# Adaptive max pooling over 16-element windows: a flat input in two groups, longer reductions, and one extra load to 16 partitions

## The chip, the cores and the metric

The kernel runs on one NeuronCore of a Trainium2 chip. The metric is the time of one execution on the device in microseconds (us). The kernel before takes 336.05 us, the median of 10 runs that lie between 335.86 and 336.18.

## The reference

The input `x` is float32 of 32 x 256 x 4096, 134.2 MB. The output is 32 x 256 x 256, 8.4 MB. Output column `i` is the maximum over 16 consecutive input elements, since 4096 / 256 = 16:

```python
for i in range(output_size):
    start = int(i * length / output_size)
    end = int((i + 1) * length / output_size)
    result[:, :, i] = np.max(x[:, :, start:end], axis=-1)
```

Every window is 64 contiguous bytes of the input and gives 4 bytes of the output. In memory both are one long row of 2,097,152 windows, so any cut of that row at a window's edge gives a valid tiling.

## The kernel before, in words

The 8192 rows of 4096 elements (16 KB each) are cut into three groups of 21 rows on each of the 128 partitions, and a rest of 128 rows, one on each partition. Within a group, partition `p` holds 21 neighbouring rows, so the distance in HBM between what two neighbouring partitions read (the pitch) is 21 x 16 KB = 336 KB.

One load (line 59, issued by SyncE, SP) brings 3 rows to each partition, 48 KB in one piece, 6,291,456 bytes in all. It goes into three of the nine places of a ring in SBUF, so the ring holds three loads. VectorE (DVE) then runs one `reduce_max` for each of the three rows (line 53): 128 partitions x 256 windows of 16 elements. The results of a group are gathered in a tile `out` of its own. There are 7 loads in a group and 21 in the three groups. The rest is one load of 16 KB to each partition (line 68), and its result goes into a place of the ring (`spare`).

The order is that of the program; the framework only adds the waits. SP issues its transfers in program order: a load waits until the reductions that read its place in the ring are done. All loads come first. After the last load SP issues the stores of the first two groups (line 72), then the third group's store in two pieces, 15 rows and 6 rows of each partition (line 74), each piece after the reductions that fill it. The 128 KB of the rest leave on ScalarE's queue (ACT, line 78). SP ends by waiting for the transfers.

Of the kernel before, what the change touches and what calls it, by code (L numbers as in the profile page):

```python
# [1 line left out]

# [4 lines left out]


@with_exitstack
def kernel(  # L10
    ctx: ExitStack,
    tc: tile.TileContext,
    x: bass.AP,
    output_size: bass.AP,
    out: bass.AP,
):

    nc = tc.nc  # L20
    P = nc.NUM_PARTITIONS
    fp32 = mybir.dt.float32

    B, C, L = x.shape
    O = int(output_size)
    assert L % O == 0, (L, O)
    W = L // O
    xf = x.flatten_outer_dims()
    of = out.flatten_outer_dims()
    rows = xf.shape[0]  # L30
    assert rows == 64 * P

    RING = 9
    G = 21
    N_GROUPS = 3
    LOAD = 3
    CUT = 15

    pool = ctx.enter_context(tc.tile_pool(name="pool", bufs=1))
    ring = pool.tile([P, RING, O, W], fp32, tag="ring", name="ring")  # L40
    outs = [
        pool.tile([P, G * O], fp32, tag=f"out{i}", name=f"out{i}")
        for i in range(N_GROUPS)
    ]

    main = N_GROUPS * G * P
    xg = xf[0:main].rearrange("(g p r) (o w) -> g p r o w", p=P, r=G, w=W)
    og = of[0:main].rearrange("(g p r) m -> g p (r m)", p=P, r=G)
    xl = xf[main:rows].rearrange("p (o w) -> p o w", w=W)
    ol = of[main:rows]  # L50

    def pooled(dst, src):
        nc.vector.reduce_max(out=dst, in_=src, axis=mybir.AxisListType.X)  # L53

    n_read = 0
    for g in range(N_GROUPS):
        for r in range(0, G, LOAD):
            at = n_read % RING
            nc.sync.dma_start(  # L59
                out=ring[:, at : at + LOAD], in_=xg[g][:, r : r + LOAD]  # L60
            )
            for i in range(LOAD):
                pooled(outs[g][:, (r + i) * O : (r + i + 1) * O], ring[:, at + i])
            n_read += LOAD

    at = n_read % RING
    spare = ring[:, (at + LOAD) % RING].rearrange("p o w -> p (o w)")[:, 0:O]
    nc.sync.dma_start(out=ring[:, at], in_=xl)
    pooled(spare, ring[:, at])

    for g in range(N_GROUPS - 1):
        nc.sync.dma_start(out=og[g], in_=outs[g])
    for a, b in ((0, CUT), (CUT, G)):
        nc.sync.dma_start(
            out=og[N_GROUPS - 1][:, a * O : b * O],
            in_=outs[N_GROUPS - 1][:, a * O : b * O],
        )
    nc.scalar.dma_start(out=ol, in_=spare)


# [1 line left out]
_INS = ['x', 'output_size']  # L82
_OUTS = [((32, 256, 256), 'float32')]

_NUMBERS = {'output_size': 256}


# [26 lines left out]
```

## Time and profile before

| | |
|---|---|
| median of 10 runs | 336.05 us |
| the profiled execution | 336.03 us |
| its span | 334.3 us |
| VectorE busy | 278.8 us, 64 reductions |
| one reduction of 128 x 4096 | 4.41 us |
| VectorE idle before loads | 47.6 us, 21 times |
| bytes moved | 142.62 MB, mean 427 GB/s |
| read from HBM, written to HBM | 134.22 MB, 8.39 MB |

The span runs from the first to the last instruction of the kernel on the core; what lies around it is the rest of the execution's time. A row of the profile's groups gives line, engine, operation, the tile written and the tile read with their shapes and a count, then the busy time in us and the mean of one in ns, then the idle time of the engine just before these instructions and what ended it. The transfers of a core are carried by 16 DMA engines. Their mean busy share is printed as tenths in 40 slices of the span. A row of a table by stretches of time gives the stretch, its length, the busy time of VectorE and GpSimd (with the number of instructions), TensorE's clock (not used here), the DMA share as a fraction of all 16 engines, and GB/s. A transfer's "time to landing" runs from its issue to the arrival of its last part.

### The profile page before, as it was taken

How to read it: one execution, taken by the hardware profiler on the slowest of the kernel's cores; microseconds unless marked ns; L12 is line 12 of the kernel's file. 1: busy time of each engine (PE TensorE's matmuls, PEld its weight loads, DVE VectorE, ACT ScalarE, POOL GpSimd, SP SyncE). 2: the span in 40 equal slices, each digit the busy share in tenths (PEclk: the TensorE clock that was granted, in tenths of full speed). 3: DMA queues.
4: the chain of work that ended last, by engine and by line, in shares of the span. 5: the costliest groups of instructions: out<-in, count | busy, mean ns of one | idle time of the engine just before them, and what ended most of it. 6: DMA issues, size and time to landing. Idle time of an engine off the chain costs nothing.

```text
span 334.3 us, 157 instructions
## 1 busy us (share of the span) xinstructions
DVE 278.8 (83%) x64; POOL 0.2 (0%) x4
## 2 busy tenths in 40 slices
DVE  0088989898898989889898898989889898988990
POOL 0000000000000000000000000000000000000000
DMA  9899898998989989899898998989989999898996
GB/s 371 382 465 465 388 465 382 465 471 382 465 382 465 471 382 465 382 465 471 382 465 388 459 471 382 465 388 454 471 388 459 394 453 471 388 459 384 444 427 294
DMA packets 3889, 142.62 MB, mean 427 GB/s; under 512 B 432, under 2 KB 560, under 8 KB 688
## 3 DMA queue, kind: packets, MB, share of 16 engines
q1 hardware_dynamic: 3744, 142.48, 98.9%
q10 hardware_dynamic: 144, 0.13, 0.1%
q14 instruction: 1, 0.01, 0.0%
HBM read 134.22 MB, written 8.39 MB: 427 GB/s over the span
## 4 chain that ended last, share of the span: by engine, by line
DMA 68%; DVE 26%; DVEq 2%; SPq 0%; issue 0%
DMA ring<-in_x_dram 68%; DVE out L53 25%; DVEq L109 2%; DVE ring L53 1%; SPq L59 0%
## 5 line engine op out<-in xcount | busy, mean ns | idle before, releaser
L53 DVE TENSOR_REDUCE out<-ring 128x256 f32<-128x4096 f32 x63 | 274.5, 4412 | 47.6 <-DMA ring<-in_x_dram 47.6
L53 DVE TENSOR_REDUCE ring<-ring 128x256 f32<-128x4096 f32 x1 | 4.4, 4409 | 0.0
L95 POOL MEMSET const-bfloat16-1.0<- 128x1 bf16 x1 | 0.1, 102 | 0.0
L95 POOL MEMSET const-uint8-127<- 128x1 uint8 x1 | 0.1, 102 | 0.0
L95 POOL MEMSET const-float32-1.0<- 128x1 f32 x1 | 0.1, 99 | 0.0
L95 POOL MEMSET const-float32-0.0<- 128x1 f32 x1 | 0.1, 98 | 0.2 <-issue 0.2
## 6 DMA issues: line engine op xcount, KB each, us to landing
ring<-in_x_dram SPq DMA_DIRECT2D x21, 6144.0 KB, 30.5
out_dram<-out SPq DMA_DIRECT2D x2, 2688.0 KB, 38.4
ring<-in_x_dram SPq DMA_DIRECT2D x1, 2048.0 KB, 29.5
out_dram<-out SPq DMA_DIRECT2D x1, 1920.0 KB, 38.2
out_dram<-out SPq DMA_DIRECT2D x1, 768.0 KB, 11.2
out_dram<-ring ACTq DMA_DIRECT2D x1, 128.0 KB, 6.4
```

What stands on the lines that cost most here:

```text
L53: nc.vector.reduce_max(out=dst, in_=src, axis=mybir.AxisListType.X)
L95: nc = _bacc.Bacc("TRN2", target_bir_lowering=False, num_devices=1)
L109: with _tile.TileContext(nc) as tc:
```

## The change

The input is taken as one flat row of windows. First 16 x 384 windows are put aside (`SIDE_P`, `SIDE`). The other 2,091,008 windows are cut into two groups of 7600 and 8736 windows on each of the 128 partitions. The pitch of a group in the input is thus 7600 x 64 B = 475 KB or 8736 x 64 B = 546 KB.

- A load brings 760 windows (47.5 KB) to each partition into one of three slots. The first group has 10 such loads, the second 11 and one of 376 windows (23.5 KB).
- One reduction pools a whole load: 128 x 760 windows in place of three of 128 x 256.
- The windows put aside are loaded before what would be the twelfth load (`SIDE_AT = 11`), into a slot of their own turn. They take two transfers on SP: 24 KB to each of partitions 0 to 14, and then the 24 KB of partition 15 written as 16 pieces of 1.5 KB. One reduction of 16 x 384 windows pools them.
- The stores all stand on SP behind the last load: the first group (128 x 7600 windows), the windows put aside (16 x 384), the second group's first 7600 windows, and its last 1136. Nothing is issued on ScalarE's queue any more.

```diff
-    RING = 9
-    G = 21
-    N_GROUPS = 3
-    LOAD = 3
-    CUT = 15
+    SLOTS = 3
+    CHUNK = 760
+
+    SIDE_P, SIDE, SIDE_AT = 16, 384, 11
+    rest = (total - SIDE_P * SIDE) // P
+    GROUPS = [10 * CHUNK, rest - 10 * CHUNK]
+    CUT = 10 * CHUNK
...
-    ring = pool.tile([P, RING, O, W], fp32, tag="ring", name="ring")
...
+    ring = pool.tile([P, SLOTS, CHUNK * W], fp32, tag="ring", name="ring")
...
+    def group(parts, n):
+
+        nonlocal taken
+        span = slice(taken, taken + parts * n)
+        taken += parts * n
+        return (
+            xw[span].rearrange("(p n) w -> p (n w)", p=parts),
+            ow[span].rearrange("(p n) -> p n", p=parts),
+        )
...
+    def next_slot(parts, n):
+        nonlocal n_loads
+        slot = ring[0:parts, n_loads % SLOTS, 0 : n * W]
+        n_loads += 1
+        return slot
...
     def pooled(dst, src):
-        nc.vector.reduce_max(out=dst, in_=src, axis=mybir.AxisListType.X)
+        nc.vector.reduce_max(
+            out=dst,
+            in_=src.rearrange("p (n w) -> p n w", w=W),
+            axis=mybir.AxisListType.X,
+        )
...
-            for i in range(LOAD):
-                pooled(outs[g][:, (r + i) * O : (r + i + 1) * O], ring[:, at + i])
...
+    def load(dst, src, a, b):
+        slot = next_slot(P, b - a)
+        nc.sync.dma_start(out=slot, in_=src[:, a * W : b * W])
+        pooled(dst[:, a:b], slot)
...
+    def load_side():
+        slot = next_slot(SIDE_P, SIDE)
+        last = SIDE_P - 1
+        nc.sync.dma_start(out=slot[0:last], in_=xs[0:last])
         nc.sync.dma_start(
...
+            out=slot[last:SIDE_P].rearrange("p (k n) -> p k n", k=16),
+            in_=xs[last:SIDE_P].rearrange("p (k n) -> p k n", k=16),
         )
-    nc.scalar.dma_start(out=ol, in_=spare)
+        pooled(side_out, slot)
+
+    stores = []
+    for g, n in enumerate(GROUPS):
+        xg, og = group(P, n)
+        o = pool.tile([P, n], fp32, tag=f"out{g}", name=f"out{g}")
+        for a in range(0, n, CHUNK):
+            if n_loads == SIDE_AT:
+                load_side()
+            load(o, xg, a, min(a + CHUNK, n))
+        for a, b in ((0, CUT), (CUT, n)):
+            if a < b:
+                stores.append((og[:, a:b], o[:, a:b]))
...
+    stores.insert(1, (os_, side_out))
+    for dst, src in stores:
+        nc.sync.dma_start(out=dst, in_=src)
```

More of the change, by code (lines that the diff above doesn't have):

```diff
@@ L27 @@
     W = L // O
[L28 to L31, printed above, removed]
-    RING = 9
-    G = 21
-    N_GROUPS = 3
-    LOAD = 3
-    CUT = 15
-    pool = ctx.enter_context(tc.tile_pool(name="pool", bufs=1))
-    ring = pool.tile([P, RING, O, W], fp32, tag="ring", name="ring")
[L41 to L47, printed above, removed]
@@ L48 @@
-    og = of[0:main].rearrange("(g p r) m -> g p (r m)", p=P, r=G)
-    xl = xf[main:rows].rearrange("p (o w) -> p o w", w=W)
-    ol = of[main:rows]
-    def pooled(dst, src):
[L53 to L61, printed above, removed]
-            for i in range(LOAD):
-                pooled(outs[g][:, (r + i) * O : (r + i + 1) * O], ring[:, at + i])
-            n_read += LOAD
@@ L66 @@
[L66 to L73, printed above, removed]
+    total = B * C * O
+    SLOTS = 3
[4 more added lines that the diff above has]
+    CUT = 10 * CHUNK
@@ new lines @@
+    pool = ctx.enter_context(tc.tile_pool(name="pool", bufs=1))
+    ring = pool.tile([P, SLOTS, CHUNK * W], fp32, tag="ring", name="ring")
+    xw = x.flatten_outer_dims().rearrange("r (o w) -> (r o) w", w=W)
+    ow = out.flatten_outer_dims().rearrange("r o -> (r o)")
+    taken = 0
+    def group(parts, n):
[6 more added lines that the diff above has]
+        )
@@ new lines @@
+    n_loads = 0
+    def next_slot(parts, n):
[3 more added lines that the diff above has]
+        return slot
+    def pooled(dst, src):
+        nc.vector.reduce_max(
[7 more added lines that the diff above has]
+        pooled(dst[:, a:b], slot)
@@ L74 @@
+    xs, os_ = group(SIDE_P, SIDE)
+    side_out = pool.tile([SIDE_P, SIDE], fp32, tag="side", name="side")
+    def load_side():
+        slot = next_slot(SIDE_P, SIDE)
+        last = SIDE_P - 1
+        nc.sync.dma_start(out=slot[0:last], in_=xs[0:last])
         nc.sync.dma_start(
-            out=og[N_GROUPS - 1][:, a * O : b * O],
-            in_=outs[N_GROUPS - 1][:, a * O : b * O],
-        )
-    nc.scalar.dma_start(out=ol, in_=spare)
+            out=slot[last:SIDE_P].rearrange("p (k n) -> p k n", k=16),
+            in_=xs[last:SIDE_P].rearrange("p (k n) -> p k n", k=16),
+        )
+        pooled(side_out, slot)
@@ new lines @@
+    stores = []
[9 more added lines that the diff above has]
+                stores.append((og[:, a:b], o[:, a:b]))
+    assert taken == total
+    stores.insert(1, (os_, side_out))
+    for dst, src in stores:
+        nc.sync.dma_start(out=dst, in_=src)
```

## The prediction

> **What bounds the kernel now.** I read the page first: busy shares, DMA bytes, the chain.
>
> ```profile
> span 334.3 us, 157 instructions
> DVE 278.8 (83%) x64; POOL 0.2 (0%) x4
> ...
> DMA  9899898998989989899898998989989999898996
> DMA packets 3889, 142.62 MB, mean 427 GB/s; under 512 B 432, under 2 KB 560, under 8 KB 688
> ...
> DMA 68%; DVE 26%; DVEq 2%; SPq 0%; issue 0%
> ...
> L53 DVE TENSOR_REDUCE out<-ring 128x256 f32<-128x4096 f32 x63 | 274.5, 4412 | 47.6 <-DMA ring<-in_x_dram 47.6
> ```
>
> VectorE (DVE) is 83% busy, and all of its idle time is waiting for loads. The DMA engines are busy in every slice. Are they the bound, or the ring? The timeline answers:
>
> ```profile
> 134.61 13.07 DVE L53 TENSOR_REDUCE out<-ring 128x256 f32<-128x4096 f32 x3 [1.46 <-DMA ring<-in_x_dram]
> 149.15 13.07 DVE L53 TENSOR_REDUCE out<-ring 128x256 f32<-128x4096 f32 x3 [1.47 <-DMA ring<-in_x_dram]
> ```
>
> One load of 6,291,456 B every 14.53 us is 433 GB/s, or 27.06 GB/s for each of 16 engines. Pooling it takes 13.07 us, so a slot is free 1.46 us before the next load lands. Issues:
>
> ```profile
> ring<-in_x_dram SPq DMA_DIRECT2D x21, 6144.0 KB, 30.5
> out_dram<-out SPq DMA_DIRECT2D x2, 2688.0 KB, 38.4
> ...
> out_dram<-ring ACTq DMA_DIRECT2D x1, 128.0 KB, 6.4
> ```
>
> 30.5 us from issue to landing is 1.46 + 14.53 + 14.53: at each issue one load is nearly done and another whole one is queued. The chain's alternation of VectorE and DMA is only how it was followed back; the engines never run dry. All 142.6 MB at 433 GB/s are 329.4 us of the 334.3 us span. The other 4.9 us lie at the ends. DMA share and GB/s (last two columns) in the last microseconds:
>
> ```profile
> 331.00:331.50 0.50, 0.00 (x0) 0.00 (x0) 1.00 1.06 432
> 331.50:332.00 0.50, 0.00 (x0) 0.00 (x0) 1.00 0.62 234
> 332.00:332.40 0.40, 0.00 (x0) 0.00 (x0) 1.00 0.09 36
> 332.40:332.90 0.50, 0.00 (x0) 0.00 (x0) 1.00 0.12 49
> 332.90:333.40 0.50, 0.00 (x0) 0.00 (x0) 1.00 0.00 0
> ```
>
> 0.12 is two engines of sixteen: two run about 1 us after the rest. The trace's sixteen completion counts per load say since when. From the first load on, one count comes 1.10 to 1.12 us after the earliest, the next-to-last at 0.29 to 0.33. After 226 us, where the one instruction fetch of the page (8 KB) holds an engine up, a second engine stands at 1.18. So an engine that is late stays late, and the last one sets the end. The trace doesn't number the engines.
>
> **What the Trainium skill says.**
> (1) "SBUF — State Buffer", section "Door 1: The DMA port swizzle": DMA bandwidth goes with the SBUF ports that the partitions reach; partitions 0 to 15 reach 4 of 16, four partitions each (0-3, 4-7, 8-11, 12-15), and were measured at 104 GB/s against 109 in the limit. Before has only transfers over 128 partitions, so its trace shows 27.06 GB/s per engine with all ports used, and nothing on the sharing of one.
> (2) "DMA: Bandwidth & Descriptors", section "Why a DMA increments its semaphore by 16 and not by 1": a transfer uses the largest k up to 16 that divides the slowest dimension, on the lowest-numbered k engines; 15 partitions would go to engines 0 to 14. Before shows k = 16 only: the 3,744 packets of SP's queue are 26 transfers x (128 rows + 16 completions).
> (3) Same page, "Latency and other measured facts": engines 7 and 15 are usually slower. The late engine agrees in kind; its number isn't to be seen.
> (4) Same section: rows at a pitch of 512 KiB copied at 207 GB/s against 214[...]. Before, at 336 KB, shows no loss.
>
> **The change part by part.** The base is the profiled execution: 336.03 us, its span 334.3 and 1.73 around it; the median is 336.05.
>
> *Flat input, 47.5 KB loads.* Loads become 128 x 48,640 B: 14.38 us at 433 GB/s. The bytes in all are the same. Pitches are 7600 x 64 B = 475 KB and 8736 x 64 B = 546 KB. Bounds: nothing, or the page's 3% of the input's 310 us (+10 us), worse by more aliasing. I take nothing: neither is a power of two.
>
> *One reduction for three.* By elements, 12160/12288 of 13.07 is 12.93 us; at worst 12160/4096 x 4.409 = 13.09. It stays 1.3 to 1.5 us under the load, as now, and hides behind it; were it over 14.38, each of 21 loads would pay the excess. VectorE has 23 reductions instead of 64; the 8 KB fetch came at about its 43rd, so I expect it gone: 0.07 us (1.18 to 1.11) where the late engine counts.
>
> *Fewer packets.* The trace's packets take 1815 ns for 49,152 B and 615 ns for 16,384 B: 15 ns each beside the bytes. Per engine: 22 x 8 + 4 x 8 + 8 = 216 before, 22 x 8 + 2 + 3 x 8 + 1 = 203 after. 13 x 15 ns: -0.2 us.
>
> *Stores.* The 128 KB one on the ACT queue goes; its bytes join three large stores and one of 24 KB on SP. Behind the last load stand two stores of 3.89 MB, 9.0 us each. The last reduction (376 windows, 6016/4096 x 4.41 = 6.5 us) starts when that before it ends, and is done some 19.4 us after load 21 lands; DMA work until then is 7.1 + 9.0 + 9.0 = 25 us. So SP's waits for the last two reductions are covered by about 6 us, as the 10.8 us wait at the end was before. Nothing but the end stands behind them on SP. Cost nothing.
>
> *The extra load.* It is two transfers on SP between full loads: 15 partitions x 24,576 B, then one partition as 16 x 1,536 B. It holds a whole slot: the load behind it is issued when reduction 9 ends, some 1.45 us before load 10 lands, and has only the extra load to cover it, not a whole one; the next full load likewise. In the first microseconds no byte moves for 1.0 us after the first issue (0.73 to 1.7), so cover is thin: 0 to 0.5 us of stall if the extra load lasts 0.9 us, none if it lasts 4. The 6.6 us reduction of the extra data makes VectorE late by about 2.5 us for two loads, under a queue that then holds 10 us or more: nothing.
>
> Its own duration is the unknown. Low bound: every engine at its own rate, 24,576/27.06 = 0.91 us. High bound: four engines write through one port. Ports 0-3, 4-7, 8-11 get 4 x 24,576 = 98,304 B: 3.63 us by the trace's rate (an estimate from the port map of page 1; by its 104 GB/s all 393 KB take 3.78). The last partition, also one port, is 0.91 us more; engines 12 to 15 get through before the others, so I take 0.5 of it (0.1 to 0.9). I choose the high bound, since page 1 reports a measured rate for this range of partitions. The queue is full at this place, so nothing hides it.
>
> Sum, with the earliest engine of load 10 as zero. Before: last engine 1.18, plus its equal share of these bytes, (384 x 16 x 68 B)/16 = 26.1 KB or 0.96 us: 2.14. After: the four engines of a port leave together at 0.1 + 3.63, whoever came late; +0.5; the 24 KB store +0.06: 4.3. Difference +2.1; packets -0.2; total +1.9. 336.03 + 1.9 = 337.9; own range 336.9 to 338.9.
>
> **Rivals.**
> *Faster: the extra load evens the engines.* If ports don't bind and the late engine is number 15, fourteen others and one more carry 24 KB extra while it carries none. For: its lag over the next, 0.79 us, nearly equals 24,576 B at 27.06 GB/s, and page 3 speaks of 15. Against: the port rate. The sum is 0.32 + 0.97 + 0.06 = 1.35 instead of 2.14, -0.8; packets -0.2; stall +0.2: 335.2. It decides if the 15-partition transfer lasts under about 1.9 us.
> *No change.* Ports don't bind, but the late engine is another, or the thin cover gives the gain back: -0.2 + 0.06 + 0 to 0.5, 336.1.
> *Slow input by its pitch.* 546 KB is near 512 KiB; a tenth of the 3% to all of it: 337 to 346, say 341. Against: the section has full rate again at 4 MiB plus 4 KiB[...].
> Another bound, VectorE, would need reductions over 14.38 us; no row speaks for it.
>
> **How the numbers follow.** Ports bind 0.62, faster 0.20, no change 0.12, pitch 0.06. A measurement can tell about 0.2% (0.67 us) from no change: 335.38 and 336.72 are the bounds. The faster case splits 0.16 faster and 0.04 same; no change gives 0.11 same and 0.01 slower; ports give 0.61 slower and 0.01 same; pitch is slower. So 0.16, 0.16, 0.68. The range 335.0 to 338.8 takes in the faster case and nearly all of the ports', and leaves out the pitch.
>
> **What would show it.** Full loads should land 14.38 us apart; reductions of 128x760 last about 12.9 us; no late fetch. Right: the full load behind the extra one lands about 18.5 us after the one before it (14.38 + 4.1), and packets of 24 KB last near 3.6 us. The faster case: about 15.4 us, packets near 0.9 us, and a last microsecond without a straggler. A stall would show as a dip of the DMA share just after the extra load. Wrong altogether: spacing other than 14.38 everywhere (pitch), or VectorE never idle.

## The result and the profile after

The changed kernel takes 339.91 us (8 runs, 339.46 to 340.20) against 336.04 us before (28 runs, 335.86 to 336.19). The ratio is 1.0115, with a 95% interval of 1.0106 to 1.0123: it is slower by 3.9 us. The forecast was 337.9 with a range up to 338.8, so the sign was right and the loss was forecast at half its size.

The profiled execution took 340.20 us with a span of 338.4, against 336.03 and 334.3: the 4.1 us between the two lie inside the span. First the page of the changed kernel: busy time, DMA shares, packets, chain, the groups of reductions, and the loads from issue to landing.

```profile
span 338.4 us, 117 instructions
DVE 281.9 (83%) x23; POOL 0.2 (0%) x4
...
DMA  9999989999998999999999999999999999999995
...
DMA packets 3664, 142.61 MB, mean 421 GB/s; under 512 B 432, under 2 KB 448, under 8 KB 576
...
DMA 63%; DVE 30%; issue 3%; DVEq 2%; SPq 0%
...
L67 DVE TENSOR_REDUCE out<-ring 128x760 f32<-128x12160 f32 (+1 forms) x22 | 275.5, 12528 | 48.0 <-DMA ring<-in_x_dram 48.0
L67 DVE TENSOR_REDUCE side<-ring 16x384 f32<-16x6144 f32 x1 | 6.5, 6529 | 0.0
...
ring<-in_x_dram SPq DMA_DIRECT2D x21, 6080.0 KB, 30.3
...
ring<-in_x_dram SPq DMA_DIRECT2D x1, 360.0 KB, 20.3
ring<-in_x_dram SPq DMA_DIRECT2D x1, 24.0 KB
```

The same bytes moved, at 421 GB/s instead of 427. VectorE is still 83% busy and still waits for loads alone, so it isn't the bound. The DMA share is no help: it is full in both kernels. A row of 48,640 B counts as a busy engine for 1.80 us where it runs freely and for up to 4.51 us where it is held up (below), so this view can't tell a working engine from a blocked one. The packet count tells something else. It is 22 loads x 128, 3 stores x 128, 16 for the small store, 15 + 1 for the extra load, and 26 x 16 + 15 + 1 completions: 3,664. The last row of the extra load is thus *one* packet of 24 KB and not 16 of 1.5 KB: the cut into 16 pieces in the source left no trace. Both sides of that transfer are contiguous; further down, with gaps on the landing side, 16 packets remain.

Where did the time go? The timeline of VectorE (start and duration in us, the operation, and in brackets the idle time before it with what ended it):

```profile
132.86 12.82 DVE L67 TENSOR_REDUCE out<-ring 128x760 f32<-128x12160 f32 x1 [1.57 <-DMA ring<-in_x_dram]
...
147.24 12.82 DVE L67 TENSOR_REDUCE out<-ring 128x760 f32<-128x12160 f32 x1 [1.55 <-DMA ring<-in_x_dram]
...
163.16 12.82 DVE L67 TENSOR_REDUCE out<-ring 128x760 f32<-128x12160 f32 x1 [3.10 <-DMA ring<-in_x_dram]
175.90 6.53 DVE L67 TENSOR_REDUCE side<-ring 16x384 f32<-16x6144 f32 x1
182.36 12.80 DVE L67 TENSOR_REDUCE out<-ring 128x760 f32<-128x12160 f32 x1
195.66 12.82 DVE L67 TENSOR_REDUCE out<-ring 128x760 f32<-128x12160 f32 x1 [0.50 <-DMA ring<-in_x_dram]
210.04 12.82 DVE L67 TENSOR_REDUCE out<-ring 128x760 f32<-128x12160 f32 x1 [1.56 <-DMA ring<-in_x_dram]
```

Everywhere else the full loads land 14.38 us apart, as forecast. From 147.24 to 195.66 three full loads and the extra one landed, in 48.42 us. Three loads are 43.14, so the extra one took 5.3 us for 0.4 MB. An equal share of its bytes on all engines would be 0.9. The first 1.5 us of this fall on the load *ahead* of it: its last completions came late, at a time when engines that had finished already carried the extra rows. Here is the DMA side of these microseconds (stretch, its length, VectorE, GpSimd, clock, DMA share, GB/s; a packet's time and bytes are counted whole in the stretch where it starts, so a share can exceed 1 and neighbouring rows swing):

```profile
160.00:161.50 1.50, 0.06 (x1) 0.00 (x0) 1.00 1.86 278
161.50:163.00 1.50, 0.00 (x0) 0.00 (x0) 1.00 0.64 130
163.00:164.50 1.50, 1.34 (x1) 0.00 (x0) 1.00 1.14 276
164.50:166.00 1.50, 1.50 (x1) 0.00 (x0) 1.00 0.27 97
166.00:168.00 2.00, 2.00 (x1) 0.00 (x0) 1.00 0.91 389
```

For 6 us the engines moved a mean of 195 GB/s, not 433: 1.43 MB too little, or 3.3 us of full rate. The trace's packets say how. The 15 rows of 24,576 B took 1.98 to 3.32 us, where 27.06 GB/s would give 0.91, and they ended between 162.4 and 164.7. The first rows of the next full load took 2.1 to 4.5 us instead of 1.80, and nearly all of them ended between 166.0 and 167.3. Even the one engine that had no row of the extra load was held up: its row of the next full load took the 4.5 us. (The trace doesn't number the engines; a row is joined here to the row that ended where it starts.) The end of the span shows the rest:

```profile
335.00:336.00 1.00, 0.00 (x0) 0.00 (x0) 1.00 0.20 77
336.00:336.50 0.50, 0.00 (x0) 0.00 (x0) 1.00 0.07 27
336.50:337.00 0.50, 0.00 (x0) 0.00 (x0) 1.00 0.05 18
337.00:337.50 0.50, 0.00 (x0) 0.00 (x0) 1.00 0.00 0
```

A share of 0.06 is one engine of sixteen. The completion counts say since when: up to the extra load the last one came 0.67 us after the first, and from it to the end 2.2 us. One engine had two packets of the extra load: it began its first row of the next full load at 166.12, when nearly all the others were ending theirs, and it never made up for it.

### The profile page after: what moved, and what is told of

It is laid out like the page before. It is cut to its first block, busy times and chain, and to the rows that moved or that the text cites. A ratio compares the mean times of both kernels' runs of the same rounds, so it can differ in the third digit from the quotient of the medians.

```text
span 338.4 us, 117 instructions
## 1 busy us (share of the span) xinstructions
DVE 281.9 (83%) x23; POOL 0.2 (0%) x4
## 4 chain that ended last, share of the span: by engine, by line
DMA 63%; DVE 30%; issue 3%; DVEq 2%; SPq 0%
DMA ring<-in_x_dram 63%; DVE out L67 28%; DVE side L67 2%; DVEq L137 2%; SPq L75 0%
## 5 line engine op out<-in xcount | busy, mean ns | idle before, releaser
L67 DVE TENSOR_REDUCE out<-ring 128x760 f32<-128x12160 f32 (+1 forms) x22 | 275.5, 12528 | 48.0 <-DMA ring<-in_x_dram 48.0
L67 DVE TENSOR_REDUCE side<-ring 16x384 f32<-16x6144 f32 x1 | 6.5, 6529 | 0.0
```

What stands on the lines that cost most here:

```text
L67: nc.vector.reduce_max(out=dst, in_=src.rearrange("p (n w) -> p n w", w=W), axis=mybir.AxisListType.X,)
```

## The experiments

Three causes were in question: the 16 neighbouring partitions share 4 ports; the extra load holds a ring slot, so the full loads behind it are issued with thin cover; the flat layout itself. The losses below are over the kernel in the first run, which is the flat layout without the extra load.

**The flat layout alone.**

```diff
-    SIDE_P, SIDE, SIDE_AT = 16, 384, 11
+    SIDE_P, SIDE, SIDE_AT = 16, 0, 99
```

The lines that make the extra group and its store go too.

> The changed kernel without the extra load (its windows go to the second group, pitch 549 KB). Ports theory (the extra load to 16 partitions makes all the loss): 335.8 us, since 13 fewer packets per engine and no late instruction fetch are left, -0.2 to -0.3. Pitch theory (the flat layout reads more slowly): near 339.9, with loads more than 14.38 us apart.

335.83 us against 335.92 of the kernel before: ratio 0.9997 (0.9988 to 1.0005). The whole loss belongs to the extra load. Pitches of 475 and 549 KB, 22 reductions instead of 64 and fewer packets make no difference that can be measured. The forecast -0.2 to -0.3 for packets and the fetch is neither confirmed nor excluded: the interval runs from -0.4 to +0.2 us.

**Fifteen rows, without the last.**

```diff
-    SIDE_P, SIDE, SIDE_AT = 16, 384, 11
+    SIDE_P, SIDE, SIDE_AT = 15, 384, 11
...
+        nc.sync.dma_start(out=slot, in_=xs)
```

> Only the transfer to partitions 0 to 14; the one to partition 15 is left out, its windows are spread over all partitions. In the profile of the change that transfer went as one packet of 24,576 B on one engine, and one engine then was 2.2 us behind the first to the end instead of 0.7. Ports theory with two parts: the lag of that one engine goes, about -1.6, so 338.3 us, and the loss of some 2.5 us over the flat kernel stays. If the loss is the slot that the extra load holds (its thin cover): unchanged, 339.9. If the last transfer makes all of it: 335.8.

338.50 us (ratio to before 1.0076, 1.0061 to 1.0091): +2.67 over the flat kernel, and 1.41 under the change. Both parts that the expectation names came near their size: 2.67 for some 2.5, and 1.41 for about 1.6. What the last row's part is made of is the next question.

**Sixteen rows in one transfer.**

```diff
-        nc.sync.dma_start(out=slot[0:last], in_=xs[0:last])
...
+        nc.sync.dma_start(out=slot, in_=xs)
```

> The same 24 KB to each of 16 partitions as one transfer, one packet for each engine. Ports theory: as with 15 partitions or a little above, 338.4 us (four full rows per port, and no engine with two). Slot theory: 339.9.

339.64 us (1.0113, 1.0097 to 1.0129; runs from 339.11 to 340.54). The expectation was missed: the sixteenth row costs about 1.1 us in this form too, though no engine carries two. Three ports carry four rows already without it, so the ports theory has nothing for it; this stays open.

**The same windows over 128 partitions, in the slot and out of it.** In the slot:

```diff
-    SIDE_P, SIDE, SIDE_AT = 16, 384, 11
+    SIDE_P, SIDE, SIDE_AT = 128, 48, 11
```

This is one transfer of 3 KB to each partition.

> The same number of windows as an extra load at the same place and in the same slot, but 3 KB to each of 128 partitions, so all ports share it. Ports theory: 335.9 us. Slot theory (the two loads behind it are issued too late): it stays above 337, with a dip of the DMA share behind the extra load.

338.18 us (1.0062, 1.0047 to 1.0077), where the ports theory said 335.9. So ports aren't the only thing that can go wrong here. The control takes the slot away and leaves all else: the data land in columns of the second group's result tile that are filled only later.

```diff
-        slot = next_slot(SIDE_P, SIDE)
+        slot = o[0:SIDE_P, n_cols - SIDE * W : n_cols]
```

> The same number of windows as 3 KB to each of 128 partitions, not in a ring slot. Neither thin cover nor shared ports: both the two-cause theory and the slot theory expect the flat kernel's time, 335.9 us. Should the place in the middle cost anything else, it stays near 338.

335.83 us (0.9997, 0.9989 to 1.0006): the flat kernel's time. The timelines side by side, first with the slot, then without. The line of SPq is the issue of the full load behind the extra one and of four after it. (The profiled execution with the slot took 337.37 us, the shortest of the four runs.)

```profile
159.83 46.23 SPq L75 DMA_DIRECT2D ring<-in_x_dram  x5
161.40 12.82 DVE L67 TENSOR_REDUCE out<-ring 128x760 f32<-128x12160 f32 x1 [1.60 <-DMA ring<-in_x_dram]
174.14 0.94 DVE L67 TENSOR_REDUCE side<-ring 128x48 f32<-128x768 f32 x1
178.50 12.82 DVE L67 TENSOR_REDUCE out<-ring 128x760 f32<-128x12160 f32 x1 [3.41 <-DMA ring<-in_x_dram]
```

```profile
145.70 58.86 SPq L75 DMA_DIRECT2D ring<-in_x_dram  x5
161.65 12.82 DVE L67 TENSOR_REDUCE out<-ring 128x760 f32<-128x12160 f32 x1 [1.59 <-DMA ring<-in_x_dram]
174.38 0.94 DVE L67 TENSOR_REDUCE side<-out 128x48 f32<-128x768 f32 x1
177.00 12.82 DVE L67 TENSOR_REDUCE out<-ring 128x760 f32<-128x12160 f32 x1 [1.67 <-DMA ring<-in_x_dram]
```

The next full load lands 17.10 us after the one ahead with the slot, and 15.35 without (14.38 plus 0.9). With the slot, the first rows of the two full loads behind the extra one took up to 2.56 and 2.96 us instead of 1.80. They were issued with 2.5 us of work or less ahead of them, at 159.83 instead of 145.70 for the first. Two engines began their first row of it at 162.56 or later, 0.7 us after the last packet of the extra load had ended: they had run dry. The engines ended 1.65 us apart instead of 0.70. A queue that is nearly dry costs about 2.3 us here (1.5 to 2.5 from run to run).

**The change without the slot.** The same edit of `slot`, with the change's two transfers:

> The change with its extra load (15 partitions, then one) in unused columns of the second group's result tile in place of a ring slot, so the full loads behind it are issued as early as ever. Two-cause theory (thin cover of the slot costs about 1.8 us, the sharing of ports the rest): 338 us. Ports alone: 339.9. Slot alone: 335.8.

340.17 us (1.0126, 1.0111 to 1.0141): no better than the change. The two-cause theory falls for this kernel. In the changed kernel's trace no engine ran dry: each one's first row of the load behind starts where its row ahead ended. While the rows hold each other up for 4 us, the late issue is covered.

**Ports: how many rows share one.** All of these are out of the slot. Sixteen neighbouring partitions in one transfer:

> 24 KB to each of 16 partitions in one transfer, not in a ring slot. Ports at 27 GB/s each (four rows of 24,576 B per port take 3.6 us instead of the 0.96 us of an equal share): 335.8 + 2.7 = 338.5, or 338 where engines that were behind lose nothing. Slot theory: 335.9.

Sixteen partitions at a step of eight; `slot` has 128 partitions here:

```diff
+        nc.gpsimd.memset(slot, 0.0)
+        nc.sync.dma_start(out=slot[0:P:8], in_=xs)
```

> The same bytes to 16 partitions at a step of eight (0, 8, ... 120), so two rows to a port by the port map instead of four; not in a ring slot; GpSimd clears the place at the start, beside the loads, and the extra reduction runs over 128 partitions. Ports theory: two rows per port take 1.8 us, so 335.8 + 0.9 = 336.7. If the cost is the number of partitions or the size of the packets and not the ports: the same as with neighbouring partitions.

Half the bytes (`SIDE = 192`) to 16 neighbouring partitions:

> As e11_own_16_in_one with 12 KB to each of 16 partitions instead of 24 KB, the rest spread over all partitions. Ports at 27 GB/s: four rows of 12,288 B take 1.8 us against an equal share of 0.5, so the loss over the flat kernel halves, from 3.2 to about 1.6: 337.4 us. If the loss is a fixed price of a transfer to few partitions: 339.0.

Fifteen partitions:

> 24 KB to each of partitions 0 to 14 in one transfer, not in a ring slot. Beside e2_15_only (338.50, in a slot) it tells what the slot adds to a transfer that lasts 3.6 us: ports alone, 338.2 to 338.5 (three of the four ports still carry four rows). Beside e11_own_16_in_one (339.05) it tells what the sixteenth row adds: if the slowest port alone counts, nothing, 339.0; if the bytes of all rows count at some 100 GB/s, -0.25.

The loss by the port map of the Trainium skill ("SBUF — State Buffer", "Door 1: The DMA port swizzle") is an estimate: rows on the fullest port x bytes / 27.06 GB/s, less the equal share of the bytes that the extra load takes off the full transfers (its input and its output).

| extra load | rows on a port | estimate | measured over 335.83 | time (runs from, to) |
|---|---|---|---|---|
| 128 x 3 KB | even | 0 | 0.00 | 335.83 (335.64, 336.09) |
| 16 x 24 KB, step 8 | 2 | 1.82 - 0.96 = 0.86 | 1.01 | 336.84 (336.55, 337.17) |
| 16 x 12 KB | 4 | 1.82 - 0.48 = 1.34 | 1.38 | 337.21 (337.01, 337.43) |
| 15 x 24 KB | 4 | 3.63 - 0.90 = 2.73 | 2.75 | 338.58 (338.33, 338.74) |
| 16 x 24 KB | 4 | 3.63 - 0.96 = 2.67 | 3.22 | 339.05 (338.19, 339.52) |

The same number of partitions and packets costs a third when they lie eight apart, and half the bytes cost half (to 0.2 us). A fixed price of a transfer to few partitions is out, and so is the number of partitions as such. The estimate fits to 0.15 us, except in the last row of the table, where it misses 0.55: a sixteenth row adds 0.47 us to fifteen out of the slot, within the scatter of its runs, and 1.1 in it. Fifteen rows cost the same out of the slot (338.58) as in it (338.50). Sixteen in one transfer took 339.05 and 339.64, with runs that overlap. The ratios to before are 1.0030 (1.0019 to 1.0040), 1.0038 (1.0025 to 1.0051), 1.0080 (1.0063 to 1.0097) and 1.0089 (1.0073 to 1.0105), in the order of the table from its second row.

**The last row.** First the change with gaps on the landing side, so that 16 pieces stay 16 packets:

```diff
-            out=slot[last:SIDE_P].rearrange("p (k n) -> p k n", k=16),
+            out=wide[last:SIDE_P].rearrange("p (k n) -> p k n", k=16)[:, :, 0:384],
```

where `wide` is the slot's first 16 x 400 columns.

> The change, but the transfer to partition 15 lands with gaps between its 16 pieces, so that they stay 16 pieces of 1,536 B, one per engine; its windows are then reduced from the wrong place (partition 15's part of the extra output is not computed rightly, the work is the same). Prediction's step as written (16 pieces cost about 0.5 us on top of the 15 partitions): near e2_15_only plus 0.5, 339.0 us, and no engine 2.2 us behind. If it is not the one packet on one engine that costs 1.4: 339.9 as the change.

339.57 us (1.0098, 1.0083 to 1.0114), but its runs lie between 338.74 and 341.01: nothing is told apart. Out of the slot the same edit scatters less. Another puts the row, as one packet, on partition 64; it has one more reduction and one more store:

```diff
+        nc.sync.dma_start(out=slot[64:65], in_=xs[last:SIDE_P])
```

> As e7_own_place (15 partitions, then partition 15, not in a ring slot), but the last row stays 16 pieces of 1,536 B, one per engine, since it lands with gaps; its windows are then reduced from the wrong place (partition 15's part of the extra output is not computed rightly, the work is the same). Step of the prediction as written: e13_15_own plus 0.1 to 0.9, 338.7 to 339.5, and no engine 2.2 us behind the first. If the row on an already shared port costs the same in any form: 340.2 as e7_own_place.

> As e7_own_place, but the last row, still one packet on one engine, goes to partition 64, whose port no other row of the extra load uses; one more reduction of 6.5 us on VectorE and one more store. Engine theory (the second packet of one engine costs it 24,576 B at its own rate, 0.9 us): 338.6 + 0.9 = 339.5, with one engine still behind. If the queueing at the shared port makes the 1.6 us of e7_own_place over e13_15_own: 338.6 to 338.9.

339.61 us (1.0108, 1.0093 to 1.0123; 339.34 to 339.96) and 339.67 us (1.0107, 1.0090 to 1.0124; 339.11 to 339.89). Over fifteen rows alone (338.58) the last row costs 1.03 us spread on a shared port, 1.09 us as one packet on a port of its own, and 1.59 us with both (340.17). Neither theory alone holds: each half is worth about 1 us, and they overlap in part. (The step from 1.0 or 1.1 to 1.6 rests on four runs each, and the intervals of the ratios overlap.) The completion counts agree: after the extra load the last engine is 1.4 us behind the first when the row is spread, 1.7 when it goes to partition 64, 2.2 when both meet, and 1.2 without the row.

**Is one engine always late?** 120 partitions give 24 KB each to 15 engines and nothing to the sixteenth, in one transfer out of the slot.

```diff
-    SIDE_P, SIDE, SIDE_AT = 16, 384, 11
+    SIDE_P, SIDE, SIDE_AT = 120, 48, 11
```

> The extra load as 3 KB to each of 120 partitions, not in a ring slot: 15 engines get 24 KB each, the sixteenth none, and no port gets more than its share. The faster rival (the highest-numbered engine is always the late one): 0.3 to 0.8 us under the same load over 128 partitions, 335.1 to 335.5. If the late engine is another one from run to run: 335.8 to 335.9.

336.88 us (1.0029, 1.0020 to 1.0039): 1.05 slower than over 128 partitions, where a gain was in question. The expectation's "no port gets more than its share" holds only over the whole load. The trace's 3 KB packets took 0.20 us on average, against 0.12 over 128 partitions, and the first rows of the next load 2.0 to 2.9 us. If each engine takes eight neighbouring partitions, then by the same port map two engines stand at one port at nearly any moment, which would cost what step 8 costs (1.01). That is argued from the size, not tested. In this run the engine that was spared had not been the last one, though eleven others had finished the load ahead before it; so whether sparing a late engine gains anything was not put to the test.

## Why the prediction was wrong

*What bounds the kernel, and the base.* Right. Loads land 14.38 us apart, a reduction takes 12.82 us (forecast 12.9), the stores and the last reductions stay covered, and the flat layout costs nothing.

*The port rate as the choice between the bounds of the extra load.* Right, and right in size: 3.63 - 0.90 is 2.73 us for fifteen rows, and the runs without the last row show 2.67 and 2.75. The port map of the Trainium skill holds in these runs, with 27 GB/s for one port, as far as neighbouring rows and a step of eight can tell. Of the two signs named for it, the full load behind landed 18.1 us after the one before it (forecast 18.5), but no packet of 24 KB lasted 3.6 us: they took up to 3.32, and the rest of the delay fell on the rows of the full loads around them.

*The term that failed first: the last row, "I take 0.5 of it (0.1 to 0.9)".* It measured 1.4 us in the slot (339.91 - 338.50) and 1.6 out of it. The step took 16 pieces on 16 engines from the source; the profile has one packet on one engine. The section of the Trainium skill that the prediction cites for k ("DMA: Bandwidth & Descriptors", "Why a DMA increments its semaphore by 16 and not by 1") has such a split spray over the engines; in this program it did so only where the landing side had gaps. As 16 pieces it would still have been about 1.0 (measured out of the slot), just over the range.

*The term that failed second: "leave together at 0.1 + 3.63, whoever came late".* This took 1.1 of the 1.18 us of lag out of the sum, as though shared ports put all engines in step. They don't: with fifteen rows the engines are 1.1 us apart after the extra load, having been 0.4 apart ahead of it, and with sixteen rows in one transfer, one to each engine, 1.0 after 0.5. So the lag of before is replaced by a new one, and the credit of 1.1 us wasn't there: fifteen rows cost 3.63 - 0.90 with nothing taken off. The two terms, 0.9 and 1.1, are the 2.0 us between 337.9 and 339.91. With the measured 1.4 for the last row, 3.63 + 1.4 - 0.96 is 4.1, as measured over the flat kernel.

*Packets -0.2 and the fetch -0.07.* The fetch is gone, as expected; the flat kernel gained 0.1, with an interval from -0.4 to +0.2 that holds the forecast and zero alike.

*Thin cover, "0 to 0.5 us of stall if the extra load lasts 0.9 us, none if it lasts 4".* The second half is right. The first is too small: 2.3 us. It took the one microsecond from the first issue to the first byte for the whole price of a dry queue. But the first rows of an execution, with nothing ahead of them, are slow too (up to 3.08 us in the kernel before, instead of 1.82), and so were those behind the short extra load.

*The rivals.* Faster is out since the ports bind. Nor did any run show one engine that is late by nature, though none put it to a clean test. In the kernel before, one stood 0.8 us behind the next; in the changed kernel three shared the last place ahead of the extra load, 0.3 us behind the rest. The pitch is out: the flat kernel reads at pitches of 475 and 549 KB as fast as before.

## What to carry to other kernels

In this kernel, whose DMA engines are always full, a small transfer was paid by its fullest port and by the engine that carries most of it, not by its bytes: 0.4 MB cost 4.1 us, and the same data as a thin slice over all 128 partitions cost nothing. In such a kernel, look at where a small transfer lands before its size. A short transfer that takes a whole slot of a ring of few slots makes the loads behind it late (2.3 us here, nothing in a place of its own). And count packets in the profile before trusting a split that is written in the source.

## What the runs showed of the hardware that was not expected

- The extra load held up an engine that had no part in it. In the changed kernel the engine without a row of it spent 4.5 us on its first row of the next load instead of 1.80, and 4.2 us with fifteen rows in the slot. Whether it waited in the fabric or for its descriptors was not separated.
- A transfer's completion can trail its data: for the load ahead of the extra one, the last three counts came 1.5 us after the last packet's end (161.5), where 0.4 to 0.5 us is usual.
- How far the last engine lags is set by the first load of an execution: the spread of the completion counts ahead of any extra load was 0.4 to 1.1 us in these profiles, and held from load to load. Each kernel has one profile, so whether it goes with the program or with the execution is not told apart. What sets it stays open, as does the scatter of the change's relatives (up to 2.3 us between runs of one kernel, where the kernel before stays within 0.5).
